# Self-attention logits of the prompt as split fp32r products, with a head's high and low query parts stacked on the 128 rows

## The chip, the cores and the metric

The kernel runs on one core of one Trainium2 chip. The metric is the device time of one execution in microseconds (us); a figure for a kernel is the median of several runs. On the core five engines work side by side, each through its own list of instructions in order: PE (TensorE, matrix products), DVE (VectorE), ACT (ScalarE), POOL (GpSimd) and SP (SyncE, which here only issues DMA transfers). They meet through semaphores. Every matrix product is two instructions: a load of the stationary operand (LDWEIGHTS, shown as PEld) and the product itself (MATMUL), which streams the moving operand's columns and adds into a PSUM bank.

## The reference, cut to what matters

One layer of a hybrid decoder for 256 prompt tokens and 8 single-token samples: a combined input projection, sliding-window attention with 16 query heads over 4 key heads, a Mamba-2 scan, an output projection, cross-attention and a convolutional FFN. The change touches the logits of the prompt's sliding-window attention alone:

```
q = rms_norm(q.reshape(b, t, N_HEADS, HEAD_DIM), w['q_norm_g'])
k = rms_norm(k.reshape(b, t, N_KV_HEADS, HEAD_DIM), w['k_norm_g'])
...
logits = jnp.einsum('bnqkgd,bnskd->bnkgqs', qb, kk, preferred_element_type=jnp.float32) * HEAD_DIM ** -0.5
...
p = sink_softmax(logits, mask[None, :, None, None], sinks...)
o = jnp.einsum('bnkgqs,bnskd->bnqkgd', p.astype(v.dtype), vv)
```

A head has 64 dimensions. The window is 128, so block 0 of the queries (128 of them) meets 128 keys and block 1 meets 256.

## The kernel before, in words

All activations lie transposed: features on the 128 partitions, the 264 tokens (256 prompt, 8 samples) along the free axis. Every large projection is done by *split products*. A value x is written as hi + lo, where hi is x rounded to the type fp32r (by ACT) and lo is x minus hi (by DVE), and the product is made of three fp32r products: hi by hi, hi by lo, lo by hi (`mm3`, L97 to L100). Weights come by DMA in parts of 128x1024 (`weights`, L72); each part is split by one ACT instruction (L85) and one DVE instruction (L86), both at high priority, and feeds 24 products. Four parts can be held. Small matrix products (attention, scan, transposes) are plain fp32.

The input projection runs in pairs of 128 output columns (`in_pair`, L331): first the pair of k, then v, then four pairs of q (L533, `jj` from 0 to 3, which fill tiles `j` = 0 to 7 of `qT`, two heads each: 64 rows a head), then the pairs of the scan's B, C and x, then z. Each pair leaves PSUM by a DVE multiplication by `r0`.

Around the change:

- L346 to L350: `kv` holds `kbd`, keys laid out in blocks: for a pair `pp` of key heads, head h stands on its own 64 rows, and the other 64 rows are zero, cleared by POOL (L350). L391 fills it on ACT, with the gain and the 1/8 in the scale. So one product of a `qT` tile (both heads on the 128 rows) with `kbd` gives both heads' logits side by side.
- L528 to L541: the squares of q go to two tiles `qsq` (tag "R", four buffers of the pool `apool`), one ACT instruction for each j (L537). Eight products with a 32-column stationary operand `nw` then sum the squares of each head into one PSUM tile `pq` (L541): for each j one with `qsq[0]`, then one with `qsq[1]`, in groups of 32 output partitions.
- L553 to L563 turn these sums into the factors 1/rms of each query.
- `attn_prompt` (L487) is called for j = 0 to 7 and does for each of the two blocks c: logits (L493), mask (L496), maximum, exponentials (L506), sums, division (L511), four or two transposes (L516 by L257), copy (L518), products with v (L522), copy into `attn` (L524). The logits use the PSUM tag "s", which has one bank.
- Tiles that share a tag share buffers. "R" is used by the input x, then `qsq`, then `xs` (L692), the scan's input. "e" (three buffers) and "xdt" (two) belong to `ssd_prompt` (L694): e is loaded by DMA (L707) and worked on by ACT (L711) only after the last attention copy. `BT` and `CT` (L660) are the scan's B and C.

The order of the instructions of each engine is fixed when the program is built: a scheduler simulates a timeline, takes what is ready by priority, and otherwise goes by the order of the program; `tc.issue_after` puts the instructions of a block behind a given one on its engine. On the chip each engine then keeps this order and waits where it must.

Of the kernel before, what the change touches and what calls it, by code (L numbers as in the profile page):

```python
# [7 lines left out]
F32 = mybir.dt.float32  # L8
F32R = mybir.dt.float32r
AF = mybir.ActivationFunctionType  # L10
ALU = mybir.AluOpType
# [5 lines left out]
TP, TS = 256, 8  # L17
# [30 lines left out]
def hybrid_decoder_step_kernel(ctx: ExitStack, tc: tile.TileContext, I, O):  # L48
    nc = tc.nc
    V, S, P, PE = nc.vector, nc.scalar, nc.gpsimd, nc.tensor  # L50
# [3 lines left out]
    apool = ctx.enter_context(tc.tile_pool(name="apool", bufs=1))  # L54
# [5 lines left out]
    def psum(tag):  # L60
        return ps.tile([128, 512], F32, tag=tag, name=tag, bufs=banks[tag])

    def T3(pool, n, dt=F32, tag=None, name=None, bufs=None):
        return pool.tile([128, n, T], dt, tag=tag, name=name or tag, bufs=bufs)
# [93 lines left out]
    def w_piece(q):  # L158
        cs = slice(512 * (q % 2), 512 * (q % 2) + 512)
        return wraw0[q // 2][:, cs], pre[q // 2][0][:, cs], pre[q // 2][1][:, cs]  # L160
# [18 lines left out]
    with tc.manual_schedule(engines={mybir.EngineType.SP, mybir.EngineType.PE, mybir.EngineType.Activation, mybir.EngineType.DVE}):  # L179
# [12 lines left out]
        raw, hi, _ = w_piece(0)  # L192
# [12 lines left out]
        for h in range(2):  # L205
            raw = raw_part()
            nc.sync.dma_start(out=raw, in_=w_in[1][:, 1024 * h:1024 * h + 1024])
            hi, lo = (wpool.tile([128, NPART], F32R, tag=t, name=t, bufs=WBUFS) for t in ("whi", "wlo"))
# [33 lines left out]
    def pc(name, i=0, n=1):  # L242
        o = _PC[name][0]
        return par[:, o + i:o + i + n]
# [10 lines left out]
    def tr(out, in_):  # L255
        k = in_.shape[0]
        PE.transpose(out, in_, cst[0:k, C_ID:C_ID + k])  # L257
# [34 lines left out]
    gq8 = cpool.tile([128, 1], F32, name="gq8")  # L292
# [21 lines left out]
    mp = mix.enter_context(tc.tile_pool(name="mp", bufs=1))  # L314
# [8 lines left out]
    def t32(name):  # L323
        return t6[:, next(t6n), :]
# [6 lines left out]
    def in_pair(evac):  # L331
        i = pair[0]
        pair[0] += 1

        if i:
            proj([w_in[2 * i], w_in[2 * i + 1]], A, evac, tag="t" if i > 13 and i % 2 else "mm")
        else:
            for m in range(2):
                with tc.high_priority():
                    evac(m, first[m][:, :T])  # L340
# [3 lines left out]
    nc.sync.dma_start(out=cpast, in_=I["cpast"])  # L344

    kv = apool.tile([128, 2080], F32, tag="B", name="kv", bufs=4)  # L346
    kbd = kv[:, 0:1024].rearrange("p (a b c) -> p a b c", a=2, b=2)
    kn = kv[:, 1024:1552].rearrange("p (a t) -> p a t", a=2)
    vT = kv[:, 1552:2080].rearrange("p (a t) -> p a t", a=2)
    P.memset(kbd, 0.0)  # L350
    kcT = apool.tile([128, 16, 129], F32, tag="B", name="kcT", bufs=4)
    nc.sync.dma_start(out=kcT, in_=I["kcT"])
    vc = apool.tile([128, 16, 128], F32, tag="B", name="vc", bufs=4)
# [10 lines left out]
    qT = attn = T3(apool, 8, tag="C", name="attn")  # L364
# [22 lines left out]
    norm_pair(r0, pc("gk"), [kn[:, m, :] for m in range(2)], blk64, 64)  # L387
    for pp in range(2):
        for h in range(2):
            hs = slice(64 * h, 64 * h + 64)  # L390
            S.activation(out=kbd[hs, pp, h, :], in_=kn[hs, pp, 0:TP], func=AF.Copy, scale=gq8[hs])  # L391
        V.tensor_copy(out=kcT[:, 8 * pp:8 * pp + 8, 128], in_=kn[:, pp, TP:T])
    nc.sync.dma_start(out=O["swa_k"], in_=kn[:, :, 128:256])
    nc.sync.dma_start(out=O["swa_ks"], in_=kcT)
# [4 lines left out]
    p = psum("y")  # L399
# [16 lines left out]
    q = t32("q")  # L416
# [16 lines left out]
    p = psum("x")  # L433
# [5 lines left out]
    p = psum("x")  # L439
# [47 lines left out]
    def attn_prompt(j, rq, nrq):  # L487
        pp = j // 4
        for c in range(2):
            nk = 128 * (c + 1)  # L490
            p = psum("s")
            s3 = p[:, 0:2 * nk].rearrange("p (h k) -> p h k", h=2)
            PE.matmul(s3, qT[:, j, c * 128:c * 128 + 128], kbd[:, pp, :, 0:nk], start=True, stop=True)  # L493
            e = mp.tile([128, 2, 256], F32, tag="h0", name="pe", bufs=3)
            ev = e[:, :, 0:nk]
            V.tensor_tensor(out=ev, in0=s3, in1=maskb[:, 256 - nk:256].unsqueeze(1).broadcast_to([128, 2, nk]), op=ALU.add)  # L496
            st = mp.tile([128, 8], F32, tag="st", name="st", bufs=4)
            mx, den, es = st[:, 0:2], st[:, 2:4], st[:, 4:6]
            V.tensor_reduce(out=mx, in_=ev, op=ALU.max, axis=AX.X)

            V.tensor_tensor(out=mx, in0=mx, in1=nrq[:, c, :], op=ALU.mult)
            V.tensor_tensor(out=mx, in0=mx, in1=nsink[:, 2 * j:2 * j + 2], op=ALU.min)
            V.tensor_tensor(out=es, in0=mx, in1=pc("sink_p", 2 * j, 2), op=ALU.add)
            S.activation(out=es, in_=es, func=AF.Exp)
            for h in range(2):
                S.activation(out=e[:, h, 0:nk], in_=e[:, h, 0:nk], func=AF.Exp, scale=rq[:, c, h:h + 1], bias=mx[:, h:h + 1],  # L506
                             accum_out=den[:, h:h + 1])
            V.tensor_tensor(out=den, in0=den, in1=es, op=ALU.add)
            V.reciprocal(out=den, in_=den)
            for h in range(2):  # L510
                V.tensor_scalar(out=e[:, h, 0:nk], in0=e[:, h, 0:nk], scalar1=den[:, h:h + 1], scalar2=None, op0=ALU.mult)  # L511
            p = psum("t")
            nb = c + 1
            for h in range(2):
                for kb in range(nb):
                    tr(p[:, (h * nb + kb) * 128:(h * nb + kb) * 128 + 128], e[:, h, kb * 128:kb * 128 + 128])  # L516
            pt = mp.tile([128, 4, 128], F32, tag="bc", name="pt", bufs=2)
            S.copy(out=pt[:, 0:2 * nb, :], in_=p[:, 0:2 * nk].rearrange("p (a q) -> p a q", q=128))  # L518
            o = psum("t")
            for h in range(2):  # L520
                for kb in range(nb):
                    PE.matmul(o[64 * h:64 * h + 64, 0:128], vn[:, kb, pp, 64 * h:64 * h + 64], pt[:, h * nb + kb, :],  # L522
                              start=kb == 0, stop=kb == nb - 1)
            marks["attn"] = S.copy(out=attn[:, j, c * 128:c * 128 + 128], in_=o[:, 0:128])  # L524

    marks = {}

    qsq = [T3(apool, 4, tag="R", name=f"qsq{i}", bufs=4) for i in range(2)]  # L528
    nw = zz[:, :, 512:544]
    for d in range(2):  # L530
        for h in range(2):
# [1 line left out]
    for jj in range(4):  # L533
        in_pair(lambda m, pm: V.tensor_tensor(out=qT[:, 2 * jj + m, :], in0=pm, in1=r0, op=ALU.mult))
        for j in (2 * jj, 2 * jj + 1):

            S.activation(out=qsq[j // 4][:, j % 4, :TP], in_=qT[:, j, :TP], func=AF.Square)  # L537
    pq = psum("s")
    for d in range(2):
        for j in range(4):  # L540
            PE.matmul(pq[32 * j:32 * j + 32, 0:TP], nw[:, d, :], qsq[d][:, j, :TP], start=d == 0, stop=d == 1)  # L541
    cpc = mp.tile([128, 24, 8], F32, name="cpc")
    ctmp = mp.tile([128, 2, TP], F32, tag="c", name="ctmp", bufs=2).rearrange("p a b -> p (a b)")[:, :192].rearrange("p (a b) -> p a b", b=8)

# [10 lines left out]
    pq = psum("x")  # L555
# [8 lines left out]
    for j in range(8):  # L564
        d = 2 * (j // 4)
        attn_prompt(j, rqs[:, :, j % 4, d:d + 2], nrqs[:, :, j % 4, d:d + 2])
# [93 lines left out]
    BT = T3(mp, 4, tag="BT")  # L660
    CT = T3(mp, 4, tag="CT")
# [14 lines left out]
    for c in range(2):  # L676
        p = psum("x")
# [4 lines left out]
    for w, XT in enumerate((BT, CT)):  # L682
        p = psum("x")
# [71 lines left out]
    p = psum("x")  # L755
# [361 lines left out]
    p = psum("y")  # L1117
# [43 lines left out]
    for pi, (wh, wl) in enumerate(weights(I["w_co"][0])):  # L1161
        wh, wl = (w.rearrange("p (k c) -> p k c", c=512) for w in (wh, wl))
        for k in range(2):
            h = 2 * pi + k
# [7 lines left out]
    for u in range(1, 4):  # L1172
        proj([I["w_co"][u]], [(OH, OL)], lambda m, pm, u=u: x2_ev(4 * u + m, pm), nb=4,
             tag=[cyc[(4 * (u - 1) + m) % 5] for m in range(4)])
# [254 lines left out]
def build(shapes):  # L1429

    import concourse.bacc as bacc

    nc = bacc.Bacc("TRN2", target_bir_lowering=False, num_devices=1)
    ins = {n: nc.dram_tensor(f"in_{n}_dram", s, dt, kind="ExternalInput").ap() for n, (s, dt) in shapes.items()}
    outs = {n: nc.dram_tensor(f"out_{n}_dram", s, F32, kind="ExternalOutput").ap() for n, s in _OUTS}
    with tile.TileContext(nc, schedule_with_timeline_sim=True) as tc:
        hybrid_decoder_step_kernel(tc, ins, outs)
    return nc
# [10 lines left out]
```

## Time and profile before

| | |
|---|---|
| median of 3 runs | 1414.26 us (1413.04 to 1414.40) |
| the profiled execution's own time | 1414.38 us |
| its span, first to last instruction | 1412.6 us (1.8 us lie around it) |
| granted TensorE clock, mean | 0.999 |
| instructions | 29090 |

The profile is of one execution. Its page has the busy time of each engine, the span in 40 slices, the DMA queues, the chain of work that ended last (followed back from the last instruction), and groups of instructions by line. The views of the trace give single instructions in order of time, tables for chosen stretches, and who waited for whom. A busy PE is modelled: products overlap, so a product of 0.28 us may start every 0.12 us, and it is the distance between starts that tells what one costs. An fp32 product shows as two MATMUL records, an fp32r product as one.

### The profile page before, as it was taken

The numbers are of one execution on the slowest core, as the hardware profiler recorded it, in microseconds if no ns is written. First come the engines' busy times: TensorE is split into PE (matmuls) and PEld (weight loads), VectorE is DVE, ScalarE is ACT, GpSimd is POOL, SyncE is SP. The second block draws the span as 40 slices with busy tenths as digits, with TensorE's granted clock in tenths as the row PEclk, the third lists the DMA queues.
The fourth block names the chain that finished last, engine by engine and source line by source line (L and its number), as shares of the span: only waits on it lengthen the run. The fifth ranks groups of instructions, "written<-read, shape, count | busy, mean of one in ns | idle before, by whom it ended". The sixth has DMA issues, their size and how long they took to land.

```text
span 1412.6 us, 29090 instructions
## 1 busy us (share of the span) xinstructions
PE 1405.0 (99%) x11547; PEld 1374.8 (97%) x11547; DVE 1048.5 (74%) x1907; ACT 767.0 (54%) x1257; POOL 93.6 (7%) x282
## 2 busy tenths in 40 slices
PE   9999999999999999999999999999999999999999
PEld 9999899999999999899999999999999999999998
DVE  7859879999997784468777775777577757765664
ACT  6647764566645554556565553555355535543432
POOL 0000001211100000020010010001000100000000
PEclk9999999999999999999999999999999999999999
DMA  8854357777767567765567675666566656655554
GB/s 290 293 179 134 116 168 243 229 248 249 238 228 252 181 208 244 261 237 189 180 226 240 236 237 181 209 237 232 183 213 228 208 181 195 197 177 190 182 190 138
DMA packets 90487, 298.32 MB, mean 211 GB/s; under 512 B 12272, under 2 KB 17264, under 8 KB 89840
## 3 DMA queue, kind: packets, MB, share of 16 engines
q1 hardware_dynamic: 84560, 277.33, 59.1%
q0 software_dynamic: 5504, 18.88, 4.1%
q8 instruction: 90, 1.47, 0.4%
q14 instruction: 45, 0.37, 0.1%
q10 hardware_dynamic: 288, 0.27, 0.1%
HBM read 280.76 MB, written 16.23 MB: 210 GB/s over the span
## 4 chain that ended last, share of the span: by engine, by line
PE 99%; DVE 0%; ACT 0%; issue 0%
PE mm L98 21%; PE mm L99 21%; PE mm L100 21%; PE t L99 10%; PE t L98 10%; PE t L100 10%; PE t L226 1%; PE s L493 1%; PE t L257 1%; PE y L727 1%; PE t L522 1%; PE y L743 0%; PE x L187 0%; PE x L257 0%; PE x L1022 0%; PE x L1051 0%
## 5 line engine op out<-in xcount | busy, mean ns | idle before, releaser
L85 ACT CAST whi<-wraw 128x1024 fp32r<-128x1024 f32 x444 | 464.6, 1048 | 526.3 <-PE mm L99 296.6
L86 DVE TENSOR_TENSOR wlo<-wraw,whi 128x1024 fp32r<-128x1024 f32 x444 | 546.1, 1231 | 240.0 <-ACT whi L85 233.9
L98 PE MATMUL mm<-x2h,whi 128*128 128x264 f32 x704 | 199.8, 284 | 0.0
L99 PE MATMUL t<-x2l,whi 128*128 128x264 f32 x704 | 199.7, 284 | 0.0
L98 PE MATMUL t<-x2h,whi 128*128 128x264 f32 x704 | 199.7, 284 | 0.0
L99 PE MATMUL mm<-x2l,whi 128*128 128x264 f32 x704 | 199.5, 284 | 0.0
L100 PE MATMUL t<-x2h,wlo 128*128 128x264 f32 x704 | 199.5, 284 | 0.0
L100 PE MATMUL mm<-x2h,wlo 128*128 128x264 f32 x704 | 199.3, 283 | 0.0
L99 PE MATMUL mm<-hl,whi 128*128 128x264 f32 x704 | 198.7, 283 | 0.0
L100 PE MATMUL mm<-hh,wlo 128*128 128x264 f32 x704 | 198.2, 283 | 0.0
L98 PE MATMUL mm<-hh,whi 128*128 128x264 f32 x704 | 197.2, 284 | 0.0
L98 PE MATMUL mm<-xh,whi 128*128 128x264 f32 x608 | 176.8, 293 | 1.8 <-DVE t L328 1.8
L99 PE MATMUL mm<-xl,whi 128*128 128x264 f32 x608 | 174.1, 288 | 0.0
L100 PE MATMUL mm<-xh,wlo 128*128 128x264 f32 x608 | 172.4, 289 | 0.0
L99 PEld LDWEIGHTS t<-x2l,whi 128*128 128x128 f32 x704 | 132.6, 188 | 0.0
L99 PEld LDWEIGHTS mm<-x2l,whi 128*128 128x128 f32 x704 | 132.5, 188 | 0.0
L99 PEld LDWEIGHTS mm<-hl,whi 128*128 128x128 f32 x704 | 132.5, 188 | 0.0
L98 PEld LDWEIGHTS t<-x2h,whi 128*128 128x128 f32 x704 | 132.5, 188 | 0.0
L98 PEld LDWEIGHTS mm<-x2h,whi 128*128 128x128 f32 x704 | 132.4, 188 | 0.0
L100 PEld LDWEIGHTS t<-x2h,wlo 128*128 128x128 f32 x704 | 132.2, 188 | 0.0
L100 PEld LDWEIGHTS mm<-x2h,wlo 128*128 128x128 f32 x704 | 132.1, 188 | 0.0
L100 PEld LDWEIGHTS mm<-hh,wlo 128*128 128x128 f32 x704 | 131.9, 188 | 0.0
(465 smaller groups left out, 2935.4 us busy)
## 6 DMA issues: line engine op xcount, KB each, us to landing
wraw<-in_w_up_dram SPq DMA_DIRECT2D x176, 512.0 KB, 4.1
wraw<-in_w_in_dram SPq DMA_DIRECT2D x102, 512.0 KB, 4.9
wraw<-in_w_dn_dram SPq DMA_DIRECT2D x88, 512.0 KB, 4.1
wraw<-in_w_out_dram SPq DMA_DIRECT2D x48, 512.0 KB, 4.3
h<-in_h_dram POOLq DMA_DIRECT2D x32, 256.0 KB, 4.8
hn<-in_h_dram SPq DMA_DIRECT2D x16, 512.0 KB, 4.9
out_state_s_dram<-hn POOLq DMA_DIRECT2D x16, 512.0 KB, 3.3
e<-dram_la SPq DMA_DIRECT2D x16, 256.0 KB, 5.1
```

What stands on the lines that cost most here:

```text
L85: S.copy(out=hi, in_=x)
L86: V.tensor_tensor(out=lo, in0=x, in1=hi.bitcast(F32), op=ALU.subtract)
L98: PE.matmul(out, wh, xh, start=start, stop=False)
L99: PE.matmul(out, wh, xl, start=False, stop=False)
L100: PE.matmul(out, wl, xh, start=False, stop=stop)
L226: PE.matmul(first[m][:, :T], w[:, m * 128:(m + 1) * 128], x, start=k + i == 0, stop=k == KB - 1 and i == 2)
L257: PE.transpose(out, in_, cst[0:k, C_ID:C_ID + k])
L493: PE.matmul(s3, qT[:, j, c * 128:c * 128 + 128], kbd[:, pp, :, 0:nk], start=True, stop=True)
L522: PE.matmul(o[64 * h:64 * h + 64, 0:128], vn[:, kb, pp, 64 * h:64 * h + 64], pt[:, h * nb + kb, :], start=kb == 0, stop=kb == nb - 1)
L727: PE.matmul(y[o:o + 64, (h // 2) * 128:(h // 2) * 128 + 128], xdt[:, h, :], es[h // 4][:, h % 4, :], start=True, stop=True)
```

## The change

The block layout `kbd` goes. In its place stand, for each pair of key heads, a tile `kh` (the scaled key rounded to fp32r, on the head's own 64 rows and copied to the other 64) and a tile `kl` (the remainder on the head's own rows, zero on the other 64). For each j and head h a tile `qs` holds the head's rounded query on its own 64 rows and its remainder on the other 64. A head's logits are then two fp32r products that add into the same place: `qs` with `kh` (high and low query by high key, over 128 rows) and `qs` with `kl` (high query by low key). So a call of `attn_prompt` makes four fp32r products for each block where it made one fp32 product for both heads.

`qs` takes all four buffers of "R"; `qsq` moves to the tags "BT" and "CT"; `kh` lies in the two buffers of "xdt" and `kl` in two of the three of "e". The eight products that sum the squares are put in another order: the one that needs the last squares (`norm(1, 3)`) comes first, the other seven are issued behind it.

```diff
     kv = apool.tile([128, 2080], F32, tag="B", name="kv", bufs=4)
-    kbd = kv[:, 0:1024].rearrange("p (a b c) -> p a b c", a=2, b=2)
...
-    P.memset(kbd, 0.0)
+
+    kh = [mp.tile([128, 2, TP], F32R, tag="xdt", name="kh", bufs=2) for _ in range(2)]
+    kl = [mp.tile([128, 2, TP], F32R, tag="e", name="kl", bufs=3) for _ in range(2)]
...
     for pp in range(2):
         for h in range(2):
-            hs = slice(64 * h, 64 * h + 64)
-            S.activation(out=kbd[hs, pp, h, :], in_=kn[hs, pp, 0:TP], func=AF.Copy, scale=gq8[hs])
+            hs, ho = (slice(64 * x, 64 * x + 64) for x in (h, 1 - h))
+            x = kn[hs, pp, 0:TP]
+            S.activation(out=kh[pp][hs, h, :], in_=x, func=AF.Copy, scale=gq8[hs])
+            S.copy(out=kh[pp][ho, h, :], in_=kh[pp][hs, h, :].bitcast(F32))
+            V.scalar_tensor_tensor(out=kl[pp][hs, h, :], in0=x, scalar=gq8[hs], in1=kh[pp][hs, h, :].bitcast(F32), op0=ALU.mult, op1=ALU.subtract)
+            P.memset(kl[pp][ho, h, :].bitcast(F32), 0.0)
...
             s3 = p[:, 0:2 * nk].rearrange("p (h k) -> p h k", h=2)
-            PE.matmul(s3, qT[:, j, c * 128:c * 128 + 128], kbd[:, pp, :, 0:nk], start=True, stop=True)
+
+            for h in range(2):
+                q = qs[j // 2][:, j % 2, h, c * 128:c * 128 + 128]
+                PE.matmul(s3[:, h, :], q, kh[pp][:, h, 0:nk], start=True, stop=False)
+                PE.matmul(s3[:, h, :], q, kl[pp][:, h, 0:nk], start=False, stop=True)
...
-    qsq = [T3(apool, 4, tag="R", name=f"qsq{i}", bufs=4) for i in range(2)]
+    qsq = [T3(mp, 4, tag=t, name=f"qsq{t}") for t in ("BT", "CT")]
+
+    qs = []
...
             S.activation(out=qsq[j // 4][:, j % 4, :TP], in_=qT[:, j, :TP], func=AF.Square)
+        qs.append(apool.tile([128, 2, 2, TP], F32R, tag="R", name=f"qs{jj}", bufs=4))
+        for j in (2 * jj, 2 * jj + 1):
+            for h in range(2):
+                hs, ho = (slice(64 * x, 64 * x + 64) for x in (h, 1 - h))
+                hi = qs[jj][hs, j % 2, h, :]
+                S.copy(out=hi, in_=qT[hs, j, :TP])
+                V.tensor_tensor(out=qs[jj][ho, j % 2, h, :], in0=qT[hs, j, :TP], in1=hi.bitcast(F32), op=ALU.subtract)
     pq = psum("s")
-    for d in range(2):
+
+    def norm(d, j):
+        return PE.matmul(pq[32 * j:32 * j + 32, 0:TP], nw[:, d, :], qsq[d][:, j, :TP], start=d == 1, stop=d == 0)
+
+
+    with tc.issue_after(norm(1, 3).ins):
+        for j in range(3):
+            norm(1, j)
         for j in range(4):
-            PE.matmul(pq[32 * j:32 * j + 32, 0:TP], nw[:, d, :], qsq[d][:, j, :TP], start=d == 0, stop=d == 1)
+            norm(0, j)
```

## The prediction, on record before the changed kernel was run

> **What bounds the kernel now.** I read the page first, then a table of stretches of the span, then single products in order of time.
>
> ```profile
> PE 1405.0 (99%) x11547; PEld 1374.8 (97%) x11547; DVE 1048.5 (74%) x1907; ACT 767.0 (54%) x1257; POOL 93.6 (7%) x282
> PE 99%; DVE 0%; ACT 0%; issue 0%
> ```
>
> PE is busy 1405.0 of 1412.6 us, and the chain that ended last is 99% PE. Busy is not yet "at its pace", so the next table (stretch; PE, PEld, DVE, ACT, POOL busy with counts of records; granted clock; DMA) is read for the distance between products.
>
> ```profile
> 36.00:39.00 3.00, 1.17 (x10) 0.99 (x9) 2.63 (x4) 1.38 (x3) 0.00 (x0) 1.00 0.67 184
> 40.00:44.00 4.00, 4.00 (x21) 3.83 (x20) 2.87 (x8) 2.98 (x5) 0.00 (x0) 0.57 0.98 379
> 40.00:98.00 58.00, 58.00 (x456) 55.48 (x455) 38.69 (x62) 29.47 (x42) 1.40 (x5) 0.97 0.74 250
> 98.00:170.00 72.00, 72.00 (x555) 63.91 (x555) 64.20 (x204) 52.70 (x132) 0.00 (x0) 1.00 0.39 125
> 216.00:400.00 184.00, 184.00 (x1533) 177.65 (x1532) 181.37 (x350) 105.39 (x186) 29.34 (x40) 1.00 0.74 242
> 660.00:900.00 240.00, 240.00 (x1984) 240.00 (x1983) 173.53 (x295) 131.68 (x212) 19.79 (x84) 1.00 0.64 212
> ```
>
> From 660 to 900 us there are only fp32r products of 264 columns: 240/1984 = 0.121 us from start to start. The lines around the logits below keep that same distance, with nothing missing between products. So PE is at its pace in the attention stage too, and time taken off PE there comes off the end, as long as no other engine becomes late. DVE has 19.3 us free in 40 to 98 and 7.8 us in 98 to 170, but only 2.6 us in 216 to 400.
>
> **What the old logits cost.** The attention's logits for block 1 (512 columns: two heads by 256 keys) and block 0 (256 columns), in PE's order of time (start, duration):
>
> ```profile
> 101.75 0.28 PE L100 MATMUL mm<-xh,wlo 128*128 128x264 f32 x1
> 101.87 1.02 PE L493 MATMUL s<-kv,attn 128*128 128x512 f32 x2
> ...
> 102.85 0.28 PE L99 MATMUL mm<-xl,whi 128*128 128x264 f32 x1
> ...
> 105.89 0.28 PE L100 MATMUL mm<-xh,wlo 128*128 128x264 f32 x1
> 106.01 0.59 PE L493 MATMUL s<-kv,attn 128*128 128x256 f32 x2
> ...
> 106.56 0.28 PE L99 MATMUL mm<-xl,whi 128*128 128x264 f32 x1
> ```
>
> Three lines take turns, L98, L99, L100, so L100 to the next L99 (its L98 is left out here) would be two distances, 0.24 us. It is 1.10 with the 512-column logits and 0.67 with the 256-column ones, so they cost 0.86 and 0.43 us: 1.68 ns a column, and no change-over on top. Eight of each: 8 x (0.86 + 0.43) = 10.3 us.
>
> **What the new logits cost.** Block 1 has four fp32r products of 256 columns. Such products stand in the cross-attention's v:
>
> ```profile
> 602.84 0.28 PE L99 MATMUL mm<-wlo,mh 128*128 128x256 f32 x1
> ...
> 604.50 0.28 PE L98 MATMUL mm<-whi,mh 128*128 128x256 f32 x1
> ```
>
> These are the first and the last of 15, so 14 distances: 1.66/14 = 0.1186 us. Four cost 0.474 instead of 0.86, eight blocks save 8 x 0.386 = 3.09 us.
>
> Block 0 has four fp32r products of 128 columns, and the trace has no fp32r product under 256 columns. Bounds: if the stream of columns alone counts, 0.1186/2 = 0.059 each; four are 0.237 and save 8 x (0.43 - 0.237) = 1.54 us. If an fp32r product this narrow goes at the pace of fp32, 128 x 1.68 ns = 0.215 each; four are 0.86 and lose 8 x 0.43 = 3.44 us. Between them lies the load of the stationary operand, which every product has. A product of one column shows it bare:
>
> ```profile
> 535.64 0.28 PE L100 MATMUL mm<-x1h,wlo 128*128 128x264 f32 x1
> 535.76 0.28 PE L969 MATMUL y<-cst,sq 128*128 128x1 f32 x2
> ...
> 536.11 0.28 PE L99 MATMUL mm<-x1l,whi 128*128 128x264 f32 x1
> ```
>
> 0.47 us instead of 0.24 for two records of a single column: 0.115 us each for a 128x128 operand. I take this value, since the load of 128 columns is the same as in the fp32r products and cannot be longer than their 0.1186. Four cost 0.46: nothing is won in block 0, 8 x 0.03 = 0.24 us is lost. Halving the columns of a product whose load takes as long buys nothing.
>
> The Trainium skill's page "TensorE: Matmul & The Clock Gate", section "LDWEIGHTS (loading the stationary operand)", states that the load takes its columns divided by 1.2 GHz, 107 ns for 128. The trace's 115 ns agrees roughly, and by 107 the loss of 0.24 would be none. The same page, "Back-to-back issue gap", gives about 81 ns for sustained pairs of load and 128-column product; by that block 0 would win 8 x (0.43 - 0.324) = 0.85 us, an estimate that the 115 ns speaks against.
>
> **The sums of squares.** Eight products on groups of 32 output partitions; now they come in three places:
>
> ```profile
> 89.69 0.28 PE L100 MATMUL mm<-xh,wlo 128*128 128x264 f32 x1
> 89.90 1.06 PE L541 MATMUL s<-qsq,zz 128*32 128x256 f32 x12
> 90.89 0.39 PE L98 MATMUL mm<-xh,whi 128*128 128x264 f32 x1
> 91.11 0.28 PE L99 MATMUL mm<-xl,whi 128*128 128x264 f32 x1
> ...
> 93.53 0.28 PE L98 MATMUL mm<-xh,whi 128*128 128x264 f32 x1
> 93.75 0.62 PE L541 MATMUL s<-qsq,zz 128*32 128x256 f32 x2
> ...
> 94.52 0.28 PE L100 MATMUL mm<-xh,wlo 128*128 128x264 f32 x1
> 94.73 0.62 PE L541 MATMUL s<-qsq,zz 128*32 128x256 f32 x2
> ...
> 95.51 0.28 PE L99 MATMUL mm<-xl,whi 128*128 128x264 f32 x1
> ```
>
> Again each pair of neighbours would be two distances apart. The six together cost 91.11 - 89.69 - 0.24 = 1.18 us, the seventh 94.52 - 93.53 - 0.24 = 0.75, the eighth 95.51 - 94.52 - 0.24 = 0.75: 2.68 us. With all eight behind `norm(1, 3)` they can run as one block. Twelve records took 0.99 us (89.90 to 90.89), 0.0825 each, and 0.19 for coming and going; sixteen give 1.32 + 0.19 = 1.51, a gain of 1.17 us. Bounds: nothing, if the build breaks the block up again; 1.5, if four column groups fill as well as the first eight records may have.
>
> **What is added beside PE.** Rows for like instructions (no 64x256 form is there except the first; I take the 128-partition rows):
>
> ```profile
> L391 ACT ACTIVATE kv<-kv,gq 64x256 f32<-64x256 f32 x4 | 2.0, 505 | 0.0
> L93 ACT CAST hh<-c 128x256 fp32r<-128x256 f32 x44 | 17.7, 402 | 0.8 <-DVE c L1261 0.8
> L93 DVE TENSOR_TENSOR hl<-c,hh 128x256 fp32r<-128x256 f32 x44 | 18.4, 419 | 0.0
> L95 DVE SCALAR_TENSOR_TENSOR yl<-xs,gssd,yh 128x256 fp32r<-128x256 f32 x16 | 7.7, 478 | 2.0 <-ACT yh L94 2.0
> L537 ACT ACTIVATE qsq<-attn x8: 401/410/418, 55.4 to 91.2; 128x256 f32<-128x256 f32 x8
> ```
>
> ACT keeps its four scalings and gets 16 + 4 copies, 20 x 0.40 = 8.0 us; DVE gets 16 differences and 4 remainders, 16 x 0.42 + 4 x 0.48 = 8.6 us; POOL trades one clear for four smaller ones. All of it falls in 40 to 98 us, where ACT is busy 29.5 and DVE 38.7 of 58. It fits, and the split weights that PE needs go ahead of it by priority, so I cost it at nothing. Were 8.6 us pushed past 170, where DVE is nearly full, the 2.6 us free in 216 to 400 would not hold it, and up to 6 us would come out on PE.
>
> The moved tiles need their buffers free in time:
>
> ```profile
> L493 PE MATMUL s<-kv,attn x32: 377/486/595, 98.5 to 169.7; 128*128 128x256 f32 x16, 128*128 128x512 f32 x16
> L648 ACT ACTIVATE xs<-c x8: 620/628/635, 180.6 to 305.6; 128x512 f32<-128x512 f32 x8
> L648 ACT ACTIVATE BT<-c x2: 620/626/631, 113.1 to 130.6; 128x512 f32<-128x512 f32 x2
> L711 ACT ACTIVATE e<-e,la x64: 385/389/405, 186.5 to 377.0; 128x128 f32<-128x128 f32 x64
> ```
>
> `xs` (buffers of `qs`) is first written at 180.6 and `e` first worked on at 186.5, after the last logits at 169.7; `BT` at 113.1, after the squares' last reading near 95. The added waits: SP's loads of `e` behind the release of `kl` (its last reading ends at 169.7, 16.8 us before the work on `e` starts; SP's weight loads queue behind it, with four parts of 24 x 0.121 = 2.9 us in hand), and PE's block of sums behind the last square, with all of PE's products queued behind that.
>
> **The sum.** 3.09 - 0.24 + 1.17 = 4.0 us off the profiled execution's 1414.38: 1410.4. The median shown is 0.12 lower, so 1410.3 for the median. A measurement here tells some 0.2% from no change, 2.8 us, so faster means under 1411.4 and slower over 1417.1.
>
> **The rivals.** (1) Narrow fp32r products go at fp32's pace: 3.09 - 3.44 + 1.17 = 0.8 us, 1413.4, no change. For it: no row shows fp32r under 256 columns. Against: load and columns, as far as rows show them, explain no such jump. (2) The change does only part of what it says: the sums of squares are broken up again. Then 2.85 us, 1411.4, on the edge. (3) Slower: PE reaches the block of sums before the last square is there. When the last q leaves PSUM, ACT has this before it:
>
> ```profile
> 90.00 0.43 DVE L534 TENSOR_TENSOR attn<-mm,r 128x264 f32<-128x264 f32 x1 [0.34 <-PE mm L100]
> L85 ACT CAST whi<-wraw 128x1024 fp32r<-128x1024 f32 x444 | 464.6, 1048 | 526.3 <-PE mm L99 296.6
> ```
>
> If two casts of weights (1.05 each) and eight copies (0.40) stood ahead of the two squares (0.41), the last would end at 90.43 + 2.1 + 3.2 + 0.8 = 96.5, and PE, there at 89.8, would stand 6.7 us. The table of stretches shows what follows a stand: after 1.8 us without products in 36 to 39 the granted clock is 0.57 in 40 to 44, 4 x 0.43 = 1.7 us more. So -4.0 + 6.7 + 1.7 = +4.4, 1418.7. It decides from a stand of about 5 us on. Against: in the program the squares come ahead of the pair's copies. The Trainium skill's page "TensorE: Matmul & The Clock Gate", section "Part 1: The HAM clock gate", puts the fall to half clock on an idle window of about 3.4 us; by that a stand of 1.8 us would have cost no clock, and the row shows a lower one right behind it. (4) DVE late after 170: up to +6 on a gain of 4.0, 1416.3.
>
> **How the numbers follow.** The forecast has 0.51, rival 1 0.28, rival 2 0.08 (half of it faster, half no change), rival 3 0.06, rival 4 0.07 (0.05 no change, 0.02 slower). Faster 0.55, same 0.37, slower 0.08. The range goes from 1409.0 (half of the bound of 1.54 us for block 0 and the 1.5 for the sums) to 1414.6 (rival 1 without the gain on the sums: 1414.26 + 0.35); the likeliest case's own is 1409.0 to 1411.5.
>
> **What would show it.** After the change, four fp32r products of 256 columns should stretch PE's neighbours by about 0.47 us and four of 128 by 0.46; distances of 0.21 would be rival 1, of 0.06 the other bound. The sixteen records of the sums should stand in one block with about 1.5 us, and PE should not stand before it. DVE and ACT should be about 8 us busier before 98 us, with PE's distances unchanged. A stand of PE with a clock under 1.0 that before has not, or DVE at its limit with wider distances, would make the forecast wrong.

## The result, and the profile after

| | before | after |
|---|---|---|
| median | 1413.65 us (1412.70 to 1414.40, 4 runs) | 1425.20 us (1423.02 to 1425.76, 4 runs) |
| the profiled execution's own time | 1414.38 us | 1425.71 us |
| its span | 1412.6 us | 1423.7 us |
| granted clock, mean | 0.999 | 0.995 |

The ratio is 1.0076, with a 95% interval of 1.0064 to 1.0088. The changed kernel is slower by 11.5 us, where a gain of 4.0 us was forecast.

**The part of PE that was forecast came about.** PE's order of time in the changed kernel, for block 1, for block 0, and for the sums of squares:

```profile
109.76 0.28 PE L100 MATMUL mm<-xh,wlo 128*128 128x264 f32 x1
109.88 0.28 PE L501 MATMUL s<-kh,qs 128*128 128x256 f32 x1
...
110.48 0.28 PE L99 MATMUL mm<-xl,whi 128*128 128x264 f32 x1
...
113.51 0.28 PE L100 MATMUL mm<-xh,wlo 128*128 128x264 f32 x1
113.63 0.22 PE L501 MATMUL s<-kh,qs 128*128 128x128 f32 x1
...
114.20 0.28 PE L99 MATMUL mm<-xl,whi 128*128 128x264 f32 x1
```

```profile
101.81 0.28 PE L98 MATMUL mm<-xh,whi 128*128 128x264 f32 x1
102.03 0.64 PE L559 MATMUL s<-qsqCT,zz 128*32 128x256 f32 x8
102.48 0.61 PE L559 MATMUL s<-qsqBT,zz 128*32 128x256 f32 x8
...
103.26 0.28 PE L100 MATMUL mm<-xh,wlo 128*128 128x264 f32 x1
```

Read as in the prediction (neighbours would be two distances, 0.24 us, apart), block 1 costs 0.72 - 0.24 = 0.48 us, block 0 costs 0.69 - 0.24 = 0.45, and the sums stand in one block of 1.45 - 0.24 = 1.21. Against before that is 8 x (0.86 - 0.48) + 8 x (0.43 - 0.45) + (2.68 - 1.21) = 4.35 us less work on PE; 4.0 was forecast.

**The loss is standing time and clock.** A *stand* is a time in which an engine runs nothing because its next instruction waits. From the page of the changed kernel, the busy line and the chain that ended last:

```profile
PE 1405.3 (99%) x11579; PEld 1379.8 (97%) x11579; DVE 1055.5 (74%) x1927; ACT 775.4 (54%) x1277; POOL 93.1 (7%) x285
PE 95%; DVE 2%; DMA 1%; ACT 1%; issue 1%; SPq 0%; DVEq 0%; ACTq 0%
```

PE is as busy as before with less to do, since a product counts as longer at a lower clock; but the chain is no longer 99% PE. Who PE waited for, in the changed kernel (us in total, times, longest):

```profile
PE y L274 <- DVE accy L845: 4.8, 1, 4.8
PE mm L98 <- DVE attn L545: 4.7, 2, 3.5
```

Neither line is there before. Where they fall, in stretches (PE, PEld, DVE, ACT, POOL busy with counts; granted clock; DMA), the changed kernel:

```profile
40.00:55.00 15.00, 11.53 (x67) 11.19 (x66) 12.50 (x26) 6.47 (x10) 1.94 (x7) 0.73 0.61 252
55.00:75.00 20.00, 18.74 (x149) 18.12 (x149) 15.50 (x33) 14.93 (x25) 0.00 (x0) 0.98 0.65 210
430.00:460.00 30.00, 25.18 (x193) 24.79 (x193) 19.58 (x33) 13.47 (x17) 0.00 (x0) 0.94 0.65 223
```

and before:

```profile
40.00:55.00 15.00, 15.00 (x110) 14.77 (x109) 13.87 (x23) 10.76 (x16) 0.00 (x0) 0.89 0.76 264
430.00:460.00 30.00, 30.00 (x251) 30.00 (x250) 23.39 (x31) 18.22 (x21) 0.00 (x0) 1.00 0.71 241
```

In front PE loses 3.47 + 1.26 us of standing, and (0.89 - 0.73) x 15 = 2.4 and (1.00 - 0.98) x 20 = 0.4 us of clock: 7.5 us. At 433 to 460 it loses 4.8 us of standing and (1.00 - 0.94) x 30 = 1.8 of clock: 6.6. The sum is -4.35 + 7.5 + 6.6 = +9.8; the profiled executions differ by 11.3. Of the rest, 0.8 us is PE's standing between 200 and 400 us, 0.4 us a longer wait near 630 us (`ohl`), and 0.3 us is not accounted for.

**The first loss: a buffer that comes late.** `kv`, the two caches `kcT` and `vc` and the zero tile `zz` share the four buffers of tag "B" with `t6` and others. Whoever is first in the fixed order gets a free one. POOL, then DVE, in the kernel before (in order of time):

```profile
25.07 0.96 POOL L350 MEMSET kv<- 128x1024 f32 x1 [24.13 <-DVE sw L307]
71.03 1.02 POOL L357 MEMSET zz<- 128x1088 f32 x1 [45.00 <-PE x L257]
```

```profile
38.87 0.75 DVE L395 TENSOR_TENSOR kv<-mm,r 128x264 f32<-128x264 f32 x2
```

and in the changed kernel:

```profile
44.16 1.01 POOL L358 MEMSET zz<- 128x1088 f32 x1 [42.62 <-DVE ctmp L575]
```

```profile
63.21 0.77 DVE L400 TENSOR_TENSOR kv<-mm,r 128x264 f32<-128x264 f32 x2 [0.80 <-ACT dsm L476]
```

The clear of `kbd` was also `kv`'s claim on a buffer, at 25 us. Without it `kv` is first written by the copy of the v pair out of PSUM (L395 before, L400 now). By then `zz` has a buffer and `kv` has none until ACT's last reading of `t6` (`dsm`, L476). The v pair waits in two of the three PSUM banks of "mm" from 39 to 63 us, so the q pairs have one bank, and PE stands for both copies of the first q pair (L545, at 49.87 and 59.53 us; the first came late on DVE too, behind two reciprocals that took 3.44 us).

**The second loss: the order of the gate.** `gate_sample` makes the samples' share of `accy`, and PE sums `accy` (L274) right behind the last output product of the attention. A *cast* is ACT's rounding of a weight part (L85), its *low part* DVE's subtraction (L86), an *eviction* a DVE instruction that takes a product's result out of PSUM (L889 for the output product); the *samples' split* makes hi and lo of the gate's result (`yh`, `yl`, L93). Casts that start before the gate's tanh on ACT, and low parts that start before the sum over `accy` on DVE, are grouped rows of a window that ends there. Before:

```profile
L85 ACT CAST whi<-wraw 128x1024 fp32r<-128x1024 f32 x116 | 120.9, 1046 | 88.2 <-PE mm L99 59.8 <-PE t L99 10.8 <-DMA wraw<-in_w_in_dram 8.3
L86 DVE TENSOR_TENSOR wlo<-wraw,whi 128x1024 fp32r<-128x1024 f32 x118 | 146.1, 1239 | 22.0 <-ACT whi L85 21.7
```

After:

```profile
L85 ACT CAST whi<-wraw 128x1024 fp32r<-128x1024 f32 x120 | 125.1, 1046 | 96.8 <-PE mm L99 59.7 <-PE t L99 22.7 <-DMA wraw<-in_w_in_dram 5.7
L86 DVE TENSOR_TENSOR wlo<-wraw,whi 128x1024 fp32r<-128x1024 f32 x120 | 146.4, 1221 | 29.1 <-ACT whi L85 28.9
```

Four more casts and two more low parts now come first (each count is one higher in the program, where one cast goes into another tile). Only four parts can be held, so the last of them waits until PE is at the last products ahead of its own sum. In the changed kernel, ACT, then DVE, then PE:

```profile
432.85 1.04 ACT L85 CAST whi<-wraw 128x1024 fp32r<-128x1024 f32 x1 [1.67 <-PE t L99]
435.39 0.31 ACT L842 ACTIVATE zsam<-zsam 128x128 f32<-128x128 f32 x1 [1.49 <-DVE ysam L841]
```

```profile
433.93 1.23 DVE L86 TENSOR_TENSOR wlo<-wraw,whi 128x1024 fp32r<-128x1024 f32 x1 [0.95 <-ACT whi L85]
435.07 0.28 DVE L841 TENSOR_TENSOR ysam<-ysam,zsam 128x128 f32<-128x128 f32 x1
437.27 0.38 DVE L845 TENSOR_REDUCE accy<-ts 128x8 f32<-128x128 f32 x1
```

```profile
437.71 0.97 PE L274 MATMUL y<-accy,cst 128*128 128x264 f32 x2 [4.82 <-DVE accy L845]
```

PE's last product frees the buffer, ACT casts, DVE subtracts, only then come the gate's last steps, the last evictions and the sum. In the kernel before, `accy` was done at 425.16 + 0.40 = 425.6 and PE came for it at 428.7, 3.1 us later:

```profile
L820 DVE TENSOR_REDUCE accy<-ts x1: 399/399/399, 425.2 to 425.2; 128x8 f32<-128x128 f32 x1
L274 PE MATMUL y<-accy,cst x2: 385/385/385, 428.7 to 428.9; 128*128 128x264 f32 x2
```

### The profile page after: what moved, and what is told of

It reads as the page before. It is cut to its first block, busy times and chain, and to the rows that moved or that the text cites. A ratio compares the mean times of both kernels' runs of the same rounds, so it can differ in the third digit from the quotient of the medians.

```text
span 1423.7 us, 29196 instructions
## 1 busy us (share of the span) xinstructions
PE 1405.3 (99%) x11579; PEld 1379.8 (97%) x11579; DVE 1055.5 (74%) x1927; ACT 775.4 (54%) x1277; POOL 93.1 (7%) x285
## 4 chain that ended last, share of the span: by engine, by line
PE 95%; DVE 2%; DMA 1%; ACT 1%; issue 1%; SPq 0%; DVEq 0%; ACTq 0%
PE mm L98 21%; PE mm L99 20%; PE mm L100 20%; PE t L98 9%; PE t L99 9%; PE t L100 9%; PE t L226 1%; DVE wlo L86 1%; PE t L257 1%; PE t L531 1%; DMA cpast<-in_cpast_dram 0%; PE y L752 0%; ACT whi L85 0%; PE y L768 0%; DMA ti<-dram_la 0%
## 5 line engine op out<-in xcount | busy, mean ns | idle before, releaser
L85 ACT CAST whi<-wraw 128x1024 fp32r<-128x1024 f32 x444 | 464.5, 1048 | 531.4 <-PE mm L99 296.7
L86 DVE TENSOR_TENSOR wlo<-wraw,whi 128x1024 fp32r<-128x1024 f32 x444 | 544.4, 1227 | 248.2 <-ACT whi L85 246.1
```

Source lines behind the costliest of these rows:

```text
L85: S.copy(out=hi, in_=x)
L86: V.tensor_tensor(out=lo, in0=x, in1=hi.bitcast(F32), op=ALU.subtract)
```

## The experiments

"Claim" is an early first write of `kv`; the "gate's order" is that of the steps above. Each ratio is to the kernel before on the same chip, whose median was 1413.7 to 1414.2 us.

| run | median, us | ratio to before, 95% interval |
|---|---|---|
| e1 claim restored | 1417.46 | 1.0024 (1.0015 to 1.0033) |
| e2 before, late clear | 1420.96 | 1.0047 (1.0033 to 1.0061) |
| e3 before, new order of sums | 1419.72 | 1.0037 (1.0025 to 1.0050) |
| e4 claim, old order of sums | 1416.87 | 1.0019 (1.0010 to 1.0028) |
| e5 claim, multiplies on POOL | 1411.26 | 0.9983 (0.9975 to 0.9992) |
| e6 before, multiplies on POOL | 1418.06 | 1.0032 (1.0020 to 1.0045) |
| e7 after, multiplies on POOL | 1418.65 | 1.0035 (1.0022 to 1.0047) |
| e8 = e3, multiplies on POOL | 1412.89 | 0.9991 (0.9982 to 1.0000) |
| e9 claim, DVE's order alone | 1419.22 | 1.0044 (1.0030 to 1.0058) |
| e10 before, accy put late | 1415.95 | 1.0020 (1.0011 to 1.0028) |
| e11 = e9 with a small claim | 1420.04 | 1.0045 (1.0033 to 1.0058) |
| e12 = e9 with old sums | 1420.78 | 1.0050 (1.0037 to 1.0063) |
| e13 claim, gate's order | 1410.46 | 0.9977 (0.9968 to 0.9986) |
| e14 after, gate's order | 1417.49 | 1.0021 (1.0012 to 1.0030) |
| e15 = e13 with a small claim | 1411.11 | 0.9980 (0.9970 to 0.9989) |
| e16 = e13 with old sums | 1411.77 | 0.9987 (0.9978 to 0.9996) |
| e17 before, gate's order | 1414.15 | 1.0004 (0.9995 to 1.0013) |
| e18 = e3, gate's order | 1413.65 | 0.9998 (0.9989 to 1.0007) |

**e1 and e2: the claim, put back and taken away.** e1 is the changed kernel with a clear nobody needs; e2 is the kernel before with its clear moved to where the keys are made, zero halves only:

```diff
     vT = kv[:, 1552:2080].rearrange("p (a t) -> p a t", a=2)
+    P.memset(kv[:, 0:1024], 0.0)
```

```diff
-    P.memset(kbd, 0.0)
...
+            P.memset(kbd[ho, pp, h, :], 0.0)
             S.activation(out=kbd[hs, pp, h, :], in_=kn[hs, pp, 0:TP], func=AF.Copy, scale=gq8[hs])
```

> The changed kernel with one line more: kv's first 1024 columns are cleared by POOL at the place where kbd was cleared before; nothing reads them. Theory A (the clear was what gave kv its buffer of the tag B early; without it zz takes that buffer, kv waits for t6, the v pair stays in PSUM and PE stands): the stand at 40 to 58 us goes, PE's first logits come near 98 us instead of 106, and the time falls by 8 us at least; if the second stand near 433 us is only its echo, by 15 us, to 1409 to 1411; if that stand has its own cause, to about 1417. Theory B (the 8 us each of new work on DVE and ACT before 98 us make the split weights late): the stand stays, 1424 to 1426.

> The kernel before, with kbd's clear moved behind the norms of k (the zero halves alone, in the loop that fills kbd), so that POOL no longer touches kv early; the fp32 logits stay. Theory A: kv loses its early buffer here too, the v pair is evicted near 63 us instead of 39, and the time rises by 8 us from the front alone, to 15 with an echo near 430 us: 1421 to 1428. Theory B: nothing is added on DVE or ACT, so no change, 1413 to 1415.

e2, with the fp32 logits untouched, loses 7.2 us (1420.96 against 1413.72, at the lower edge of what Theory A gave): `zz` takes the buffer at 44.0 us, the v pair is copied at 61.6, and PE stands 3.2 us for the q pair's copy (`attn`, L534).

```profile
44.02 1.01 POOL L356 MEMSET zz<- 128x1088 f32 x1 [43.09 <-DVE ctmp L550]
```

In e1 the v pair is copied at 38.6 us, and the stand for `attn` is gone; what remains is the other one, with a clock of 0.97 and 0.91 around it:

```profile
PE y L274 <- DVE accy L846: 4.8, 1, 4.8
```

```profile
400.00:430.00 30.00, 25.18 (x202) 24.49 (x201) 26.38 (x51) 13.36 (x21) 0.55 (x1) 0.97 0.70 220
430.00:460.00 30.00, 30.00 (x227) 29.79 (x228) 19.52 (x29) 15.89 (x21) 0.00 (x0) 0.91 0.59 200
```

So the front loss is the claim, in both directions, and the second loss is a cause of its own, not an echo of the first.

**e3 and e4: the order of the sums, alone and taken out.** e3 is the kernel before with only the new `norm`; e4 is e1 with the old loop over `d` and `j`.

> The kernel before with only the new order of the eight products that sum the squares. As PE's distances in the changed kernel read (1.21 us for the block against 2.68 in three places) 1.47 us are won: 1412.1 to 1412.5. If PE's time there is not on the path, no change.

> As e1_claim, with the old order of the eight products that sum the squares. It should lie 1.2 to 1.5 us above e1_claim if the block of sums is worth what PE's distances say, and stand 2.9 us below the kernel before for the logits alone if no stand is left.

Both missed. e3 should have gained a little and lost 6.0 us, with a new stand:

```profile
PE y L274 <- DVE accy L827: 3.8, 1, 3.8
```

A change of the order of eight small products at 90 us made a stand at 430 us, and in e4 it is there as well (3.2 us). In the traces of e3 and e4 120 casts lie ahead of the tanh, as in the changed kernel. So either half of the change by itself was enough to give the gate its late place in the order.

**e5 to e8: DVE's work before the gate reduced.** The same edit on e1, before, after and e3:

```diff
-                V.tensor_tensor(out=h0, in0=h0, in1=cb, op=ALU.mult)
+                (P if g == 3 else V).tensor_tensor(out=h0, in0=h0, in1=cb, op=ALU.mult)
```

> The changed kernel with the claim of the buffer restored (as in the run that cleared the first 1,024 columns of kv early), and with the eight multiplies of the samples' states of group 3 on POOL instead of DVE. This takes 8 x 0.68 = 5.4 us from DVE ahead of the samples' gate and puts the last sum of the gate (accy) two low-part subtractions earlier in DVE's order. Theory A (the 4 us that the split products save are lost because PE stands at the sum over accy, which DVE reaches too late in its fixed order): no stand at that sum, PE keeps its lead, and the time is 1409.0 to 1411.0 us, 2.7 to 4.5 below the kernel before. Theory B (the lead is lost whatever DVE does, in the clock or in the weights that come from memory): still 1416 to 1418 us, with the same loss at another wait.

> The kernel before with the same eight multiplies on POOL. Control. In the kernel before PE reaches the sum over accy 2.9 us after DVE is done and stands nowhere there. Theory A: no gain, 1413.0 to 1414.2 us. If DVE's load holds PE back all along (Theory C: DVE is the bound of the whole stage from 98 to 430 us), it gains 2 us or more.

> The changed kernel as it is (claim not restored) with the same eight multiplies on POOL. Theory A: only the loss ahead of the logits (7 us, the v pair that waits for its buffer) remains, less the 4 us that the products and sums save: 1425.2 - 6.7 = 1418.5 us, range 1416.5 to 1419.5, and no stand at the sum over accy. Theory B: 1425.

> The kernel before with only the new order of the sums of squares, and the same eight multiplies on POOL. It was 1419.7 us without the move to POOL, with 3.8 us of stand at the sum over accy. Theory A: the stand goes and the 1.2 us of the sums are cashed: 1412.4 us, range 1411.5 to 1413.5. Theory B: 1419 to 1420.

Three times the stand at L274 went and 6 to 7 us came back (1417.46 to 1411.26, 0.3 above the range given; 1425.2 to 1418.65; 1419.72 to 1412.89). The control e6 missed: 4.3 us slower, where nothing was to be gained or lost. PE stood there for the low part of the attention's output, and these rows of DVE and POOL show why:

```profile
PE mm L99 <- DVE atl L93: 3.6, 1, 3.6
```

```profile
376.75 1.50 DVE L95 SCALAR_TENSOR_TENSOR yl<-xs,gssd,yh 128x256 fp32r<-128x256 f32 x1
378.17 1.91 DVE L804 SCALAR_TENSOR_TENSOR xs<-th,xs 128x256 f32<-128x256 f32 x1
380.00 1.24 DVE L93 TENSOR_TENSOR atl<-attn,ath 128x1056 fp32r<-128x1056 f32 x1
...
381.77 2.34 DVE L93 TENSOR_TENSOR atl<-attn,ath 128x1056 fp32r<-128x1056 f32 x1
```

```profile
376.40 1.55 POOL L771 TENSOR_TENSOR h<-h,cb 128x512 f32<-128x512 f32 x1 [5.66 <-DMA cb<-dram_bc]
...
378.51 1.28 POOL L771 TENSOR_TENSOR h<-h,cb 128x512 f32<-128x512 f32 x1
381.71 1.28 POOL L771 TENSOR_TENSOR h<-h,cb 128x512 f32<-128x512 f32 x1 [1.92 <-DMA h<-in_h_dram]
```

Instructions that take 0.47, 0.41 and 1.24 us elsewhere took 1.50, 1.91 and 2.34 while POOL's multiply ran. Of the 3.6 us, (1.50 - 0.47) + (1.91 - 0.41) = 2.5 are this: they lie ahead of the first `atl`, for which PE waited until 381.3. The rest is not worked out.

These four runs leave open whether DVE had too much to do or only the wrong order, since the edit changes both.

**e9, e11, e12: DVE's order alone.** No work moves; the low parts of the weight parts behind the attention's output product (the 118th to the 123rd) are ordered behind the sum over `accy`. e11 has the same on a claim of 8 columns, e12 on e4.

```diff
+    lows, late = [], []
+    NPART, WBUFS = 1024, 4; pin = lambda: tc.issue_after(late[0]) if late and len(lows) in range(117, 123) else ExitStack()
...
+                with pin(): lows.append(V.tensor_tensor(out=lo, in0=x, in1=hi.bitcast(F32), op=ALU.subtract))
...
+        late.append(V.tensor_reduce(out=accy[:, TP:], in_=t.rearrange("p k b -> p b k"), op=ALU.add, axis=AX.X).ins)
```

> The changed kernel with the claim of the buffer restored and no work moved between engines: only the low-part subtractions of the four weight parts that follow the attention's output product are ordered on DVE behind the samples' sum over accy. PE's order is the same as in the run that restored the claim alone (1417.5 us). Theory A1 (the stand is made by the order: accy lies behind low parts that need a buffer which PE gives back only right ahead of its own sum over accy): no stand of PE at that sum, 1409.3 to 1411.3 us. Theory A2 (DVE simply has too much work before accy): little changes, 1415.5 to 1417.5 us, since DVE has as much to do as before.

> As the run with the order of accy mended, but the early claim of the buffer is a clear of 8 columns instead of 1,024. If the front loss comes from who takes the buffer and not from the time of POOL's clear, the time is that of that run within 0.5 us: 1409.3 to 1411.3 us. If the length of the clear mattered, the v pair's copy would come late again and it would be 1416 us or more.

> The claim restored, the order of accy mended, but the sums of squares in their old order: the split products alone. PE's rows give the products 8 x (0.86 + 0.43) - 8 x (0.45 + 0.48) = 2.9 us of saving, so 1410.8 us if all of it is cashed, range 1410.0 to 1412.0 us, and 1.2 to 1.5 us above the run with the new order of the sums if that too is cashed. If DVE's lateness takes it, no difference between the two.

All three missed, at 1419 to 1421 us. In e9 `accy` was ready in time and PE did not stand for it; it stood behind it instead:

```profile
PE mm L98 <- ACT yh L93: 4.4, 1, 4.4
PE mm L99 <- DVE yl L93: 1.8, 1, 1.8
```

```profile
427.07 0.48 ACT L261 ACTIVATE ry<-y,eps 128x264 f32<-128x264 f32 x1
429.33 0.39 ACT L93 CAST yh<-ysam 128x64 fp32r<-128x64 f32 x2 [1.77 <-DVE ysam L847]
```

`ry` had come ahead of the samples' split on ACT, and that split's input (L847) stood on DVE behind three of the low parts that I had put back and four evictions. Here it was not enough to mend one engine's order.

**e10: the reverse.** The kernel before, with the one sum over `accy` ordered behind the last output product's evictions (the call of the gate stands later in the program for this, and the products that follow are held behind PE's sum); the orders of PE and ACT are unchanged.

```diff
-        V.tensor_reduce(out=accy[:, TP:], in_=t.rearrange("p k b -> p b k"), op=ALU.add, axis=AX.X)
+        with tc.issue_after(last[0]): V.tensor_reduce(out=accy[:, TP:], in_=t.rearrange("p k b -> p b k"), op=ALU.add, axis=AX.X)
...
+            last[0] = V.tensor_tensor(out=x, in0=pm, in1=x, op=ALU.add).ins
```

> The kernel before, PE's and ACT's order and all work unchanged; only the one 0.4 us sum over accy is ordered on DVE behind the four evictions of the last output product, so behind PE's last product ahead of the sum. Theory A1: PE stands there for the evictions and the sum, 4 x 0.34 + 0.39 = 1.8 us and a little, some 2 to 3 us, and if the clock falls after it as it did after the stand in the changed kernel, up to 3.6 us more: 1415.5 to 1419 us. Theory A2: DVE has the same work, the time stays at 1413.2 to 1414.2 us.

2.05 us lost by the place of one instruction of 0.4 us:

```profile
429.82 0.71 PE L274 MATMUL y<-accy,cst 128*128 128x264 f32 x2 [1.36 <-DVE accy L820]
```

**e13 to e18: the gate's order on both engines.** The casts from the 119th on come behind the tanh, from the 121st behind the samples' split; low parts from the 120th, and the last evictions, behind the split on DVE; `ry` behind the split on ACT. (`late` holds the samples' two splits, each as ACT's and DVE's instruction; the rule ends with the 123rd part.) No work moves.

```diff
+    NPART, WBUFS = 1024, 4; pin = lambda a=0: tc.issue_after((late[1][1] if not a else marks["tanh"] if len(lows) < 120 else late[1][0]).ins) if late and 119 - a <= len(lows) < 123 else ExitStack()
...
+                with pin(1): S.copy(out=hi, in_=x)
+                with pin(): lows.append(V.tensor_tensor(out=lo, in0=x, in1=hi.bitcast(F32), op=ALU.subtract))
...
+            with tc.issue_after(late[1][1].ins) if late and i >= 6 else ExitStack(): V.tensor_tensor(out=x, in0=pm, in1=x, op=ALU.add)
...
+    with tc.issue_after(late[1][0].ins): ry = total(accy, 4 * D, "ry")
```

> The changed kernel with the claim restored, and with the order mended on both engines, no work moved: on ACT the casts of the weight parts from the 119th on come behind the gate's tanh (it stood behind 121 of them, in the kernel before behind 117) and the later ones behind the samples' split; on DVE the low parts from the 120th on and the last four evictions come behind the samples' split. The run that mended DVE alone had accy ready in time but put the samples' split behind ry on ACT. Theory A1 (order): no stand of PE at the sum over accy nor at yh or yl behind it, 1409.0 to 1411.5 us. Theory A2 (too much work on DVE ahead of accy): a stand of 3 us or more stays there, 1415 us or more.

> The changed kernel with its late claim left as it is, and the same mended order of the gate on ACT and DVE. Theory A1: the front loss of 7 us stays and the stand goes, 1417.5 to 1419.5 us. Theory A2: 1423 us or more.

> As the run with the claim restored and the order mended on both engines, but with an early clear of 8 columns of kv instead of 1,024. If the claim and not the length of POOL's clear decides the front: the time of that run within 0.5 us. If the length mattered: 5 us or more above it.

> Claim restored, order mended on both engines, but the sums of squares in their old order: the split products alone. PE's rows give them 2.9 us: 1410.5 to 1412.5 us, and 1.2 to 1.5 us above the run that has the new order of the sums as well. If no difference shows, the sums' saving is lost elsewhere.

> Control: the kernel before with the same rule for the order of the gate. It has nothing to mend there (the tanh stays behind 117 casts, accy behind 119 low parts). If the 3.8 us that the changed kernel gains with claim and order mended come from the split products and the new order of the sums, this stays at the time of before, 1413.2 to 1414.7 us. If the ordering itself were worth something, it would be 1 us or more below.

> The kernel before with only the new order of the sums of squares (1419.7 us as built, with a stand at accy) and the gate's order mended, no work moved. Theory A1: the stand goes and the sums' 1.2 to 1.5 us are cashed, 1412.2 to 1413.2 us. Theory A2 (DVE's work): 1418 us or more.

e13, DVE and then PE:

```profile
421.86 0.41 DVE L846 TENSOR_REDUCE accy<-ts 128x8 f32<-128x128 f32 x1
```

```profile
425.17 0.61 PE L274 MATMUL y<-accy,cst 128*128 128x264 f32 x2
```

`accy` is done 2.9 us before PE comes; PE comes 3.5 us earlier than in the kernel before (428.7) and does not stand. At 1410.46 us it is the fastest of all. With the two causes set apart (medians, us):

| | gate as built | gate's order mended |
|---|---|---|
| `kv` late (the change) | 1425.20 | 1417.49 |
| `kv` claimed early | 1417.46 | 1410.46 |

Each cause costs 7.0 to 7.7 us and they add. e17 shows that the same rule is worth nothing to the kernel before (1414.15 against 1413.77). It has little to move there, one low part and the four evictions on DVE and nothing on ACT, so it shows that e13's 3.8 us are not a gain of the rule itself. e15: with a clear of 8 columns the front is as good (1411.11, 0.65 above e13 where 0.5 was allowed; the ranges, 1409.2 to 1414.9 and 1409.1 to 1414.2, lie over each other). So the claim counts and not the length of the clear. e16 is 1.3 us above e13, the sums' share as expected. e18 lost the stand (1419.72 to 1413.65), but the sums' gain of 1.2 us doesn't show in its median, within an interval of 1.6 us below before to 1.0 above; in its profile PE comes to L274 at 427.4, 1.3 us before the kernel before.

## Why the prediction was wrong

- **The terms of the sum held.** Block 1 was 0.48 for 0.474 us, block 0 was 0.45 for 0.46, the sums 1.21 for 1.51: 4.35 us instead of 4.0. Rival 1 (narrow fp32r products at fp32's pace) and rival 2 (the sums broken up again) fell. The Trainium skill's page "TensorE: Matmul & The Clock Gate", "Back-to-back issue gap", with about 81 ns for a pair of load and 128-column product, would have given 0.32 us for block 0, an estimate; the four took 0.45, so here the measurement decides for 0.11 us each, the pace of the one-column product in the prediction.
- **First step that failed:** "POOL trades one clear for four smaller ones", costed at nothing, and "the moved tiles need their buffers free in time". I followed the tags that tiles were moved to (R, BT, CT, e, xdt) and not the tag of the tile that lost its first writer. The clear of 0.96 us was `kv`'s place in the queue for "B"; e1, e2 and e13 against e14 show that its absence costs 7.0 to 7.7 us, e15 that the claim does it and not the clear's length.
- **Second step that failed:** "time taken off PE there comes off the end, as long as no other engine becomes late". Right as a condition, but I weighed it by DVE's free time alone (rival 4: late after 170 us by too much work, 0.07). DVE was late at 430 us by its order, behind casts that wait for PE itself, and PE stood 4.8 us for `accy`. In e13 and e14 the work is that of e1 and after, and 7.0 to 7.7 us came back. Rival 4 had the right place of decision and the wrong cause, and with +6 on a gain of 4.0 it was still 9 us short.
- Rival 3 (PE stands at the block of sums) did not come: no wait there. The sign that the prediction named, a stand of PE with a clock under 1.0 that the kernel before has not, came twice.
- With both causes out, the change gives 1410.46 us, 3.8 less than the kernel before by the medians (by the ratio 3.3, 95%: 2.0 to 4.5); 1410.3 was forecast. That they lie 0.2 us apart is in part luck: PE's distances give 4.35 us and not 4.0, and the interval is wide. The forecast was of the arithmetic, not of the program the scheduler built.
- Why the scheduler places the gate behind 120 casts rather than 116 is not settled: it did so in the changed kernel, in e3 and in e4 alike. Which order would come was not in the profile of before. What could have been read there is the reserve of 3.1 us at L274, less than one cast, one low part, four evictions and a sum take (1.05 + 1.23 + 4 x 0.34 + 0.4 = 4.0 us).

## What to carry to other kernels

Before removing a write, ask whether it was a tile's first one: in a shared pool it is also the claim on a buffer, and the next claimant moves up. With an order fixed at build, follow the few places where PE needs the end of a serial chain of other engines, and note its reserve there; if the chain is placed behind work that needs a buffer from PE, PE's gain comes back as a stand, whatever the busy shares say. When an edit moves the time by more than it touches, look for a new wait far away, and restore the old order there before judging the edit.

## What the runs showed of the hardware

- **A stand can cost clock after it.** Behind the stand of 4.82 us, products of 264 columns came every 0.22 us instead of 0.12:

```profile
439.14 0.42 PE L100 MATMUL mm<-yh,wlo 128*128 128x264 f32 x1
439.36 0.42 PE L98 MATMUL mm<-yh,whi 128*128 128x264 f32 x1
...
441.34 0.34 PE L99 MATMUL mm<-yl,whi 128*128 128x264 f32 x1
```

  From 437.71 to 441.34 that is 3.6 us at about half pace. The Trainium skill's page "TensorE: Matmul & The Clock Gate", section "Part 1: The HAM clock gate", puts the return from half to full clock behind a busy window of about 3.4 us, and the trace agrees. Behind e10's stand of 1.36 us only the next product came late (0.32 us), the rest every 0.12. Behind e4's stand of 3.22 us at L274 the granted clock was 1.00 (428 to 438 us), while behind the 1.83 us that PE of the kernel before stands ahead of 38.74 us it was 0.57 in 40 to 44. So the length of a stand alone does not tell whether clock is lost.
- **Beside POOL's multiply DVE took longer.** The rows under e6. The Trainium skill's page "SBUF — State Buffer", section "SBUF: two separate sides", states that DVE's instructions with two SBUF inputs and GpSimd's share a pair of ports under an exclusive lock for a whole instruction. The trace agrees as far as three instructions can show it: DVE's excess was 1.03, 1.50 and 1.10 us beside multiplies of 1.28 to 1.55. Work moved from DVE to POOL is therefore not free for DVE.
